# Half-precision pairs for the products with normed activations, their weight scales measured a tile behind, and a piecewise end of the layer outputs

## The chip, the cores and the metric

One core of a Trainium2 chip runs the whole program, four transformer layers in one launch. The metric is the device time of one execution in microseconds. TensorE (PE) does the matrix products, VectorE (DVE) and ScalarE (ACT) the element work, GpSimd (POOL) some of it, SyncE (SP) issues nearly all DMAs.

## What is computed

512 latent tokens of width 1024 pass two layers of a first block and two of a second; in the first layer of the first block 256 context tokens go along, so it works on 768 columns. All in fp32 accuracy. Cut to what the change touches:

```python
# first block, l = 0, 1
u  = modulate(rms_norm(h, g_norm1[l]), ...)            # 1024 wide
pl = u @ w_in[l]                                       # 2720 columns: three kinds of attention
gates = sigmoid(u @ w_gate[l] + b_gate[l])             # 3072 columns
h  = h + mod * (sum(gates * branches) @ w_o[l])
u2 = modulate(rms_norm(h, g_norm2[l]), ...)
h  = h + mod * conv_ffn(u2, w_up[l], ..., w_down[l])   # 5632 up columns, 2816 down rows
# second block, l = 0, 1
proj = rmsnorm(x, attn_norm_w[l]) @ w_in_2[l]          # 2964 columns: state space, short conv, sparse attention
x = x + concat([y_ssd, y_sc, y_nsa]) @ w_out_2[l]
u = causal_dwconv(rmsnorm(x, ffn_norm_w[l]) @ ffn_w_up_2[l], ...)   # 5504 columns
x = x + (silu(gate) * val) @ ffn_w_down_2[l]
```

## The kernel before

Activations lie transposed: 128 rows of d on the partitions (eight tiles for 1024), tokens along the free dimension, in columns 0 to 511 for the latent tokens and 512 to 767 for the context. Below, F0 and F1 are the two layers of the first block (class `First`) and N0 and N1 those of the second (class `Second`).

**Products.** Every dense product is made of three matmuls, since each fp32 operand x is held as a pair of float32r tiles, hi and lo = x - hi: `mm3` (L200) issues wh*xh and wh*xl for all k, then wl*xh. A product of a 128-column weight tile with 1024 rows over 512 tokens is thus 24 matmuls of 512 columns. In the trace a normed activation is `uh`/`ul`, a weight pair `wh`/`wl`, the inner activations of the feed-forward part `hh`/`hl`. The attention weights against values (`pt`, `v`) are fp16 pairs already.

**Weights.** `WS.get` (L660) loads 256 columns (1 MB) into one of two buffers `wr`, and splits 128 columns at a time: ACT copies to `wh`, DVE subtracts to `wl`; there are three buffers of each. In the mixers of the second block (`g.wpool = 1`) POOL does the subtraction.

**Norm.** `Norm.run` (L548) takes a function `tile(k, piece)` that makes output tile k of the preceding product. It does tiles 0 to 6 whole, adding their squares to one sum (`full`); the last tile is done piece by piece of 256 tokens, and after each piece `chain` sums the squares over the partitions on PE, takes the root on POOL, and spreads it over the partitions with PE; `scale` then makes the pairs `uh`/`ul`. `Between` is the norm from F1 to N0 (two norms in one), `Finish` the last one with the output.

**Feed-forward** (`ffn`, L1481). Groups of four 128-row tiles: `up` makes gate and value products (each evacuated by `conv_tile`: one ACT with scale and bias, two DVE taps) and a pair hh/hl; `down` multiplies the group with w_down and adds it to h. Two tiles of the next product are begun piece by piece by `early`. The pair hh/hl lies in ring `K` (14 buffers in the first block, 22 in the second, where h lies in it too).

**Order.** The order of each engine's instructions is that of a scheduler which places them by priority (program order) and a model of times; engines then run in that order, each waiting for what its next instruction needs. Products of mixers are interleaved by `weave` with attention work.

Of the kernel before, what the change touches and what calls it, by code (L numbers as in the profile page):

```python
# [18 lines left out]
P = 128  # L19
# [9 lines left out]
SPLIT = 1  # L29
# [7 lines left out]
SM = 26  # L37
UP, VP = 2.0 ** 14, 2.0 ** 12
LAT = (0, S)
# [26 lines left out]
class Gen:  # L66
    def __init__(self, tc, ins, outs, ctx, dbg=None):
# [4 lines left out]
        self.hold = []  # L72
# [27 lines left out]
    def param(self, shape, dt=F32, name="c"):  # L100
        n = int(np.prod(shape[1:]))
        tag, b = ("K128", 24) if n <= 32 else ("K512", 10)
        assert n <= 128
        return self.cp.tile(shape, dt, name=self.nm(name), tag=tag, bufs=b)
# [23 lines left out]
    def parts(self, n, name):  # L128
# [4 lines left out]
        return out  # L133

# [134 lines left out]

    def stats(self, sq, Dn, ntt, eps=EPS, bank="po", small=False):  # L270
# [187 lines left out]
class Norm:  # L458
    def __init__(self, g, h, n, A, B, parts=THIRDS):
        self.g, self.h, self.n, self.A, self.B = g, h, n, A, B  # L460
        self.u, self.rp, self.acc, self.sq = None, [], {}, {}
        self.tiles = [x for x in parts if x[0] < n]

# [59 lines left out]
    def scale(self, i, ks=range(KD)):  # L523
        g = self.g
        o, w = self.tiles[i]
        if self.u is None:
            self.u = [g.parts(self.n, "u") for _ in self.h]
        rp = self.cols(i)
        for k in ks:
# [5 lines left out]
            if b is None:  # L535
                s = g.act(y, x)
                (g.ptt if k % 3 == 2 else g.tt)(z, x, y.bitcast(F32), OP.subtract)
            else:
                s = g.act(y, x, AF.Identity, bias=b)
                if k % 2 == 1:  # L540
                    g.act(x, x, AF.Identity, bias=b)
                    g.ptt(z, x, y.bitcast(F32), OP.subtract)
                else:
                    g.stt(z, x, b, y.bitcast(F32), OP.add, OP.subtract)
        if i == 0:
            g.hold = [v, s]

    def run(self, tile, segs, split=1):  # L548
# [21 lines left out]
class Between(Norm):  # L570
    def __init__(self, g, h, g1, f):
# [4 lines left out]
        self.A = [gw]  # L576
        self.rs = g.param([P, 4], name="rsk")
# [10 lines left out]

    def chain(self, i, last):
# [3 lines left out]
        qs = [(x, 0, k) for x, k in zip(self.sq.pop(i), last)]  # L593
# [58 lines left out]
class WS:  # L652
# [7 lines left out]
    def get(self, c, M):  # L660
# [30 lines left out]
        out.key = (id(self), c)  # L691
        return out
# [235 lines left out]
class First:  # L928
    def __init__(self, g, l, h, ada_next=None):
# [4 lines left out]
        self.nq = T if self.ctxq else S  # L934

# [71 lines left out]
    def win(self, c0, c1, cc=256):  # L1007
        return self.g.wstream(self.g.I["w_in"][self.l], 0, KD, c0, c1, cc)
# [329 lines left out]
    def gates(self):  # L1338
        g = self.g
        wg = g.wstream(g.I["w_gate"][self.l], 0, KD, 0, 3 * D)  # L1340
        self.th = []

        def one(d):
            th = g.slot("L", "th")
            wt = wg.get(d * P, P)
            for o, wd in self.qsegs:
                ps = yield from g.dense(wt, self.u, (o, wd))
                g.act(th[:, o:o + wd], ps, AF.Tanh, scale=0.5, bias=self.hbg[:, d:d + 1])
# [73 lines left out]
    def project(self, merged, sp):  # L1422
# [9 lines left out]
        h, xs = [], []  # L1432

        def tile(d, sg):
            w, (o, wd) = wo.get(d * P, P), sg
# [6 lines left out]
        return h, Norm(g, h, nq, A, B).run(tile, self.qsegs)  # L1442

    def run(self, ahead, consumer):
# [16 lines left out]
        u = ffn(g, u2, h, self.qsegs, I["w_up"][l], I["w_down"][l], D_FF, self.cw, self.cb, (0, 44 // 2), 1,  # L1461
# [6 lines left out]
def conv_tile(g, ps, seg, out, cw, cb, c, lead, M):  # L1468
    o, w = seg
    nt = len(cw)  # L1470
    g.act(out[:M, o:o + w], ps, AF.Identity, scale=cw[lead][:M, c:c + 1], bias=cb[:M, c:c + 1])
    for j in range(nt):
# [5 lines left out]
        g.stt(x, ps[:, a + d:b + d], cw[j][:M, c:c + 1], x, OP.mult, OP.add)  # L1478


def ffn(g, u, h, segs, w_up, w_down, dff, cw, cb, coff, lead, scale, consumer, ahead):  # L1481
# [3 lines left out]
    wg = g.wstream(w_up, 0, KD, 0, dff)  # L1485
    wv = g.wstream(w_up, 0, KD, dff, 2 * dff)
# [3 lines left out]
    def up(ts):  # L1490
        hs = []
        for p0 in range(0, len(ts), 2):
            pair = ts[p0:p0 + 2]
            gates = []
            for t in pair:
# [3 lines left out]
                for sg in segs:  # L1499
                    conv_tile(g, drain(g.dense(w, u, sg, M)), sg, x, cw, cb, coff[0] + t, lead, M)  # L1500
                g.act(x[:M, :n], x[:M, :n], AF.Silu)
                gates.append(x)
            for t, gt in zip(pair, gates):
# [3 lines left out]
                for sg in segs:  # L1507
                    conv_tile(g, drain(g.dense(w, u, sg, M)), sg, x, cw, cb, coff[1] + t, lead, M)
                g.tt(x[:M, :n], x[:M, :n], gt[:M, :n], OP.mult)
# [6 lines left out]
    def down(ts, hs):  # L1516
        wd = g.wstream(w_down, ts[0] * P, [min(P, dff - t * P) for t in ts], 0, D, 512, 256)

        def tile(d, sg):
            o, wid = sg  # L1520
            ps = drain(g.dense(wd.get(d * P, P), hs, sg))
# [9 lines left out]
    def rest(c, hs):  # L1531
        tile = down(c, hs)
        for d in range(KD):
            for sg in segs:
                tile(d, sg)
# [699 lines left out]
```

## Time and profile before

| | |
|---|---|
| median of 3 runs | 3877.01 us (3876.66 to 3880.73) |
| the profiled execution | 3866.76 us, span 3865.0 us |
| PE, DVE, ACT, POOL busy | 96%, 64%, 46%, 13% of the span |
| mean granted TensorE clock | 0.970 |
| read from HBM, written | 339.32 MB, 38.67 MB |

The profile is read by stage. From the trace's start: F0 mixers to about 866 us, its norm and feed-forward to 1432, F1 mixers 1450 to 2104 and feed-forward 2122 to 2470, N0 mixers 2492 to 2790 and feed-forward 2806 to 3168, N1 mixers 3180 to 3478 and feed-forward 3492 to 3850, then the output. The short stretches between are norms.

### The profile page before, as it was taken

How to read it: one execution, taken by the hardware profiler on the slowest of the kernel's cores; microseconds unless marked ns; L12 is line 12 of the kernel's file. 1: busy time of each engine (PE TensorE's matmuls, PEld its weight loads, DVE VectorE, ACT ScalarE, POOL GpSimd, SP SyncE). 2: the span in 40 equal slices, each digit the busy share in tenths (PEclk: the TensorE clock that was granted, in tenths of full speed). 3: DMA queues.
4: the chain of work that ended last, by engine and by line, in shares of the span. 5: the costliest groups of instructions: out<-in, count | busy, mean ns of one | idle time of the engine just before them, and what ended most of it. 6: DMA issues, size and time to landing. Idle time of an engine off the chain costs nothing. (4 is left out here: it accounts for less than half of the span.)

```text
span 3865.0 us, 54467 instructions
## 1 busy us (share of the span) xinstructions
PE 3704.6 (96%) x20896; PEld 3078.4 (80%) x20896; DVE 2458.5 (64%) x4270; ACT 1794.8 (46%) x3000; POOL 512.0 (13%) x423
## 2 busy tenths in 40 slices
PE   8999999999999999989999999989999998999999
PEld 6888887888888888867767888767788876778886
DVE  5857676656544467668665555678765567876555
ACT  4646666424333236557654333455543335554333
POOL 2101110221000003121112000234100003410000
PEclk9999999999999999999999999989999998999999
DMA  8636898922222225559993322324433322453231
GB/s 246 145 90 153 180 218 226 244 89 79 88 77 87 72 77 131 118 136 216 232 274 126 110 95 93 94 70 104 113 100 98 96 83 67 99 132 98 88 106 60
DMA packets 692255, 483.96 MB, mean 125 GB/s; under 512 B 345790, under 2 KB 620892, under 8 KB 691996
## 3 DMA queue, kind: packets, MB, share of 16 engines
q1 hardware_dynamic: 686172, 468.33, 45.5%
q0 software_dynamic: 5824, 12.15, 1.6%
q8 instruction: 165, 2.70, 0.3%
q14 instruction: 94, 0.77, 0.1%
HBM read 339.32 MB, written 38.67 MB: 98 GB/s over the span
## 5 line engine op out<-in xcount | busy, mean ns | idle before, releaser
L176 ACT ACTIVATE wh<-w 128x1024 fp32r<-128x1024 f32 (+5 forms) x518 | 503.1, 975 | 720.3 <-PE pM L189 232.3
L179 DVE TENSOR_TENSOR wl<-w,wh 128x1024 fp32r<-128x1024 f32 (+3 forms) x464 | 526.0, 1136 | 359.8 <-ACT wh L176 99.7
L189 PE MATMUL pM<-uh,wh 128*128 128x512 f32 (+5 forms) x1832 | 687.2, 381 | 14.6 <-ACT dr L176 9.4
L189 PE MATMUL pM<-ul,wh 128*128 128x512 f32 (+5 forms) x1832 | 662.4, 375 | 0.0
L189 PE MATMUL pM<-uh,wl 128*128 128x512 f32 (+5 forms) x1832 | 450.0, 373 | 0.0
L189 PEld LDWEIGHTS pM<-uh,wh 128*128 128x128 f32 (+3 forms) x1832 | 352.3, 192 | 79.3 <-ACT dr L176 12.7
L189 PEld LDWEIGHTS pM<-ul,wh 128*128 128x128 f32 (+3 forms) x1832 | 343.4, 191 | 56.7
L189 PEld LDWEIGHTS pM<-uh,wl 128*128 128x128 f32 (+3 forms) x1832 | 327.2, 189 | 56.7
L189 PE MATMUL pT<-uh,wh 128*128 128x512 f32 (+3 forms) x912 | 311.1, 353 | 3.0 <-ACT uh L176 2.3
L189 PE MATMUL pT<-ul,wh 128*128 128x512 f32 (+3 forms) x912 | 298.2, 348 | 0.0
L176 ACT ACTIVATE p<-pS,nb 128x768 f32<-128x768 f32 (+7 forms) x304 | 217.6, 716 | 122.4 <-DVE nb L793 116.8
L793 DVE TENSOR_REDUCE nb<-pS 128x1 f32<-128x768 f32 (+7 forms) x304 | 218.0, 725 | 54.6 <-PE pS L189 52.9
L182 DVE SCALAR_TENSOR_TENSOR hl<-p,sm,hl 128x768 f16<-128x768 f32 (+5 forms) x224 | 174.2, 781 | 71.9 <-ACT hl L176 70.4
L176 ACT ACTIVATE hl<-p,sm 128x768 f16<-128x768 f32 (+5 forms) x224 | 159.9, 719 | 108.5 <-DVE sm L1297 26.2
L185 POOL TENSOR_TENSOR rs<-st,half 128x2 f32<-128x2 f32 (+2 forms) x34 | 32.3, 949 | 1327.8 <-DVE st L512 1148.9
L189 PE MATMUL pT<-uh,wl 128*128 128x512 f32 (+3 forms) x912 | 205.3, 351 | 0.0
L185 POOL TENSOR_TENSOR wl<-w,wh 128x1024 fp32r<-128x1024 f32 (+1 forms) x54 | 129.6, 2404 | 537.6 <-ACT wh L176 421.6
L189 PEld LDWEIGHTS pT<-uh,wh 128*128 128x128 f32 (+2 forms) x912 | 171.4, 188 | 28.8 <-ACT uh L176 4.3
L189 PE MATMUL po<-pt,v 128*128 128x128 f16 (+1 forms) x1656 | 174.8, 250 | 16.6 <-DMA pt<-hl 13.0
L189 PEld LDWEIGHTS pT<-ul,wh 128*128 128x128 f32 (+2 forms) x912 | 166.7, 186 | 22.5
L189 PEld LDWEIGHTS <-v 128*128 128x128 f16 x1656 | 123.3, 101 | 60.9 <-issue 43.8
L189 PEld LDWEIGHTS pT<-uh,wl 128*128 128x128 f32 (+2 forms) x912 | 153.8, 188 | 21.9 <-issue 0.4
(581 smaller groups left out, 7763.0 us busy)
## 6 DMA issues: line engine op xcount, KB each, us to landing
w<-w_up SPq DMA_DIRECT2D x44, 1024.0 KB
aw<-w_ada SPq DMA_DIRECT2D x40, 1024.0 KB
w<-ffn_w_up SPq DMA_DIRECT2D x40, 1024.0 KB
w<-w_in SPq DMA_DIRECT2D x70, 512.0 KB
w<-w_gate SPq DMA_DIRECT2D x24, 1024.0 KB
w<-w_down SPq DMA_DIRECT2D x20, 1024.0 KB
ld<-spill SPq DMA_DIRECT2D x51, 384.0 KB
w<-ffn_w_down SPq DMA_DIRECT2D x16, 1024.0 KB
```

The costliest lines, as they stand in the source:

```text
L176: return self.nc.scalar.activation(out, in_, func, **kw)
L179: return self.nc.vector.tensor_tensor(out, a, b, op=op)
L182: return self.nc.vector.scalar_tensor_tensor(out, a, s, b, op0=op0, op1=op1)
L185: return self.nc.gpsimd.tensor_tensor(out, a, b, op=op)
L189: return self.nc.tensor.matmul(out, l, r, start=start, stop=stop)
L793: nc.vector.tensor_reduce(nb, ps, axis=AX.X, op=OP.max, negate=True)
```

## The change

Four things. (1) In F1, N0 and N1 the norms write their pairs in fp16, scaled so that their bound fits (`Norm.fit`, factor `inv`), and w_in, w_gate, w_up are split into fp16 pairs scaled by a constant over the root of a bound on the matrix's sum of squares (`WS16`); the scale is undone where a product is evacuated (`dense_raw`, `conv_tile` through scaled taps, `hf`). F0, w_o, w_down, w_branch, w_out and the head products stay float32r pairs. hi and lo of a weight tile lie in one buffer, so the six buffers hold six weight tiles. (2) The scale needs the sum of squares of each weight matrix, so it is read once more ahead of its use: `Measure.steps` loads pieces of 128 rows by up to 768 columns into ring `K`, two after each tile of a feed-forward part (`next(g.slow)`), and squares or takes the maximum of each one step later, two of three on ACT, one on DVE, placed behind the last evacuation (`behind`). F1's matrices (46.8 MB) are measured in F0's feed-forward part, N0's (34.7 MB) in F1's, N1's (34.7 MB) in N0's. (3) Ahead of the four norms that follow a feed-forward part, four output tiles instead of one are done piece by piece (`SPLIT = 4`), in the second block's middle norms two instead of one. (4) In the mixers of the second block the weight subtraction goes from POOL to DVE, products rotate over pM, pT, pM (four banks) instead of pM (two), and `conv_silu` evacuates by `conv_tile` straight from PSUM instead of from a copy.

```diff
-SPLIT = 1
+SPLIT = 4
@@ Gen
+    def parts16(self, n, name):
+        lat = self.t("U", [P, S], F32, name).bitcast(F16)
+        if n == S:
+            return [lat[:, :S], lat[:, S:]]
...
     def dense_raw(self, wp, x, segs, M=P, r0=0, tag="R"):
+        f = getattr(wp, "f", None)
...
-            self.act(out[r0:r0 + M, sg[0]:sg[0] + sg[1]], ps)
+            self.tail[0] = self.act(o, ps) if f is None else self.act(o, ps, AF.Copy, scale=f[:M])
@@ Norm
+    def fit(self, gain):
...
+        for v in range(n):
+            nc.vector.tensor_reduce(m[:, v:v + 1], gain[v], axis=AX.X, op=OP.max, apply_absolute_value=True)
...
+        ps = g.bank("po")
+        for v in range(n):
+            g.mm(ps[:, :1], mb[:, v:v + 1].to_broadcast([P, P]), g.onesb[:, :1], v == 0, v == n - 1)
...
+    def part(self, k, i, key=0, scale=None):
+        g = self.g
+        o, w = self.tiles[i]
+        a = self.acc[key][:, o:o + w]
+        (g.ptt if key else g.tt)(a, a, self.square(k, o, w, scale), OP.add)
     def run(self, tile, segs, split=1):
...
                 for k in last:
                     tile(k, self.tiles[i])
-                self.sq[i] = [self.square(k, *self.tiles[i]) for k in last]
+                    if k < KD - 1:
+                        self.part(k, i)
+                self.sq[i] = [self.square(KD - 1, *self.tiles[i])]
+class Measure:
...
+    def behind(self, e, f):
+        g = self.g
+        with ExitStack() as st:
+            if g.tail[e] is not None:
+                st.enter_context(g.tc.issue_after(g.tail[e].ins))
+            f()
+    def steps(self):
...
+        def square(i, x):
+            g.act(x, x, AF.Square, accum_out=acc[:, i:i + 1])
+        def largest(i, x):
+            a = acc[:, i:i + 1]
+            nc.vector.tensor_reduce(a, x, axis=AX.X, op=OP.max, apply_absolute_value=True)
+            g.tt(a, a, a, OP.mult)
+        for i, (k, a, b) in enumerate(cuts):
+            x = g.slot("K", "wm")[:, :b - a]
+            nc.sync.dma_start(x, self.w[k * P:(k + 1) * P, a:b])
+            todo.append((i, x))
+            if len(todo) == 2 or i == n - 1:
+                yield
+                for j, y in todo:
+                    e = int(j % 3 == 2)
+                    self.behind(e, lambda: (square, largest)[e](j, y))
+                todo = []
...
+class WS16:
...
+    def split(self, raw, n):
+        g = self.g
+        g.ws += 1
+        pr = g.t("wh" if g.ws % 2 else "wl", [P, 2, KD, n], F16, "w2")
...
+            g.act(pr[:, 0], raw, AF.Copy, scale=self.m.s)
+            g.stt(pr[:, 1], raw, self.m.s, pr[:, 0], OP.mult, OP.subtract)
@@ ffn, after each tile of up and each d of a group's down
+                next(g.slow, None)
...
+    drain(g.slow)
     out = consumer(h).run(down(cs[-1], b), segs, SPLIT)
@@ Second
     def conv_silu(self, c, j, tag):
-        ps = yield from g.dense_raw(self.win(c, c + P).get(c, P), self.u, [LAT])
+        ps = yield from g.dense(self.win(c, c + P).get(c, P), self.u, LAT)
...
-        g.wpool = 1
+        g.wpool, g.banks = 1, MB
...
-        u2 = Norm(g, h, S, [self.gf], None).run(tile, [LAT])
+        nm = Norm(g, h, S, [self.gf], None, half=True)
+        u2 = nm.run(tile, [LAT], 2)
```

## Rows read from the trace of the kernel before

**Rows 1.** The page, busy time of each engine (share of the span, instructions).
```profile
PE 3704.6 (96%) x20896; PEld 3078.4 (80%) x20896; DVE 2458.5 (64%) x4270; ACT 1794.8 (46%) x3000; POOL 512.0 (13%) x423
```

**Rows 2.** Windows: length, busy time of each engine, clock, DMA share, GB/s.
```profile
core 0: us, PE busy (x) PEld busy (x) DVE busy (x) ACT busy (x) POOL busy (x), PEclk, DMA share, GB/s
881.00:1432.00 551.00, 551.00 (x3274) 483.36 (x3273) 294.47 (x435) 178.39 (x230) 4.60 (x5) 1.00 0.25 81
1432.00:1450.00 18.00, 15.84 (x105) 14.91 (x104) 11.73 (x35) 8.37 (x17) 4.32 (x6) 0.72 0.28 85
1450.00:2104.00 654.00, 611.94 (x3671) 498.40 (x3671) 443.59 (x798) 362.47 (x614) 123.98 (x113) 0.97 0.74 180
2122.00:2470.00 348.00, 347.00 (x1536) 287.39 (x1537) 205.05 (x263) 135.30 (x168) 6.67 (x5) 1.00 0.31 99
2470.00:2492.00 22.00, 15.12 (x90) 11.16 (x89) 14.85 (x48) 8.65 (x19) 9.09 (x11) 0.69 0.23 70
2492.00:2790.00 298.00, 269.86 (x1567) 218.88 (x1565) 222.07 (x425) 153.45 (x313) 92.25 (x53) 0.93 0.41 99
2790.00:2806.00 16.00, 13.49 (x95) 12.30 (x95) 13.61 (x35) 8.51 (x18) 5.13 (x6) 0.89 0.02 2
2806.00:3168.00 362.00, 359.47 (x1569) 288.10 (x1568) 205.27 (x270) 133.67 (x170) 0.00 (x0) 1.00 0.32 98
3168.00:3180.00 12.00, 9.64 (x57) 7.87 (x56) 7.59 (x25) 4.87 (x11) 5.18 (x5) 0.72 0.23 66
3850.00:3865.00 15.00, 7.31 (x53) 6.56 (x52) 3.56 (x7) 3.58 (x7) 1.40 (x2) 0.69 0.38 140
```

**Rows 3.** Timeline of PE: start us, us, operation, count of equal neighbours merged.
```profile
2496.62 1.12 PE L189 MATMUL pT<-ul,wh 128*128 128x256 f32 x8
2909.87 1.98 PE L189 MATMUL pT<-uh,wl 128*128 128x512 f32 x8
...
1515.60 2.14 PE L189 MATMUL po<-pt,v 128*128 128x256 f16 x18
1886.13 1.18 PE L189 MATMUL po<-pt,v 128*128 128x128 f16 x18
```

**Rows 4.** Windows again, of the instructions on tile uh alone, from F1 on.
```profile
1440.00:3865.00 2425.00, 1192.39 (x4016) 729.18 (x4016) 35.77 (x68) 43.81 (x104) 30.38 (x36) 0.96 0.44 117
2122.00:2470.00 348.00, 207.87 (x672) 126.17 (x672) 0.00 (x0) 0.00 (x0) 0.00 (x0) 1.00 0.31 99
2806.00:3168.00 362.00, 209.03 (x680) 125.35 (x679) 1.29 (x4) 0.81 (x2) 0.00 (x0) 1.00 0.32 98
```

**Rows 5.** Timeline of PE about the norm from N0 to N1, idle time before in brackets.
```profile
3169.47 1.05 PE L189 MATMUL po<-ones,sq 128*128 128x1 f32 x8
...
3175.49 0.44 PE L189 MATMUL pT<-uh,wh 128*44 128x256 f32 x1 [0.53 <-ACT uh L176]
```

**Rows 6.** Mixers of N0: a wait of PE, and timelines of POOL and DVE.
```profile
PE pM L189 <- ACT dr L176: 5.4, 3, 4.9
...
2502.53 5.20 POOL L185 TENSOR_TENSOR wl<-w,wh 128x1024 fp32r<-128x1024 f32 x2 [9.92 <-ACT wh L176]
...
2505.39 2.38 DVE L1618 TENSOR_SCALAR gates<-gates 128x48 f32<-128x48 f32 x1
2508.45 0.17 DVE L1623 TENSOR_SCALAR dz<-dx 128x32 f32<-128x32 f32 x1
```

**Rows 7.** Groups by shape over the whole trace: busy us, mean ns | idle before.
```profile
L176 ACT ACTIVATION_READ_ACCUMULATOR p<-pS,nb 128x1 f32 x304 | 58.7, 193 | 0.0
L176 ACT ACTIVATE sq<-h 128x768 f32<-128x768 f32 x22 | 18.6, 844 | 16.9 <-DVE h L182 16.7
L176 ACT ACT_TABLE_LOAD x10 | 12.8, 1283 | 2.5 <-DVE gt L182 1.6 <-PEq L2225 0.7
L179 DVE TENSOR_TENSOR wl<-w,wh 128x1024 fp32r<-128x1024 f32 x394 | 488.2, 1240 | 312.4 <-ACT wh L176 95.0 <-PE pM L189 78.4 <-PE pT L189 65.8
L793 DVE TENSOR_REDUCE nb<-pS 128x1 f32<-128x768 f32 x128 | 120.5, 950 | 22.9 <-PE pS L189 22.2
```

**Rows 8.** Waits of SP's queue in N0's feed-forward part: us in total, times, longest.
```profile
SPq L669 <- DVE wl L179: 307.2, 33, 20.1
```

More of the change, by code (lines that the diff above doesn't have):

```diff
@@ L592, in chain @@
         o, w = self.tiles[i]
-        qs = [(x, 0, k) for x, k in zip(self.sq.pop(i), last)]
+        qs = [(x, 0, KD - 1) for x in self.sq.pop(i)]
         for tt in range(2):
@@ new lines, with __init__, load, get @@
+class WS16:
+    def __init__(self, g, w, m, c0, c1, cc):
+        self.g, self.w, self.m, self.c1, self.cc = g, w, m, c1, cc
+        self.rawr = self.curr = (0, 0)
+    def load(self, c):
+        g = self.g
+        e = min(c + self.cc, self.c1)
+        self.raw = g.t("wr", [P, KD, e - c], F32, "w")
+        g.last = g.nc.sync.dma_start(self.raw, self.w[:, c:e].rearrange("(k p) n -> p k n", p=P))
+        self.rawr = (c, e)
+    def split(self, raw, n):
+        g = self.g
+        g.ws += 1
+        pr = g.t("wh" if g.ws % 2 else "wl", [P, 2, KD, n], F16, "w2")
+        with ExitStack() as after:
+            g.soft -= 1
+            for x in g.hold if g.soft >= 0 else ():
+                after.enter_context(g.tc.issue_after(x.ins))
+            g.act(pr[:, 0], raw, AF.Copy, scale=self.m.s)
+            g.stt(pr[:, 1], raw, self.m.s, pr[:, 0], OP.mult, OP.subtract)
+        return pr
+    def get(self, c, M):
+        if not (self.curr[0] <= c and c + M <= self.curr[1]):
+            if not (self.rawr[0] <= c < self.rawr[1]):
+                self.load(c)
+            e = min(c + P, self.rawr[1])
+            o = c - self.rawr[0]
+            self.cur, self.curr = self.split(self.raw[:, :, o:o + e - c], e - c), (c, e)
+        return self.pack(self.cur, c - self.curr[0], M, (id(self), c))
+    def pack(self, pr, o, M, key):
+        out = Wt((pr[:, 0, k, o:o + M], pr[:, 1, k, o:o + M]) for k in range(KD))
+        out.key, out.f = key, self.m.f
@@ L1007, in win, with measures, ready @@
     def win(self, c0, c1, cc=256):
-        return self.g.wstream(self.g.I["w_in"][self.l], 0, KD, c0, c1, cc)
+        g, w = self.g, self.g.I["w_in"][self.l]
+        return g.wstream16(w, self.ms["in"], c0, c1, cc) if "in" in self.ms else g.wstream(w, 0, KD, c0, c1, cc)
+    def measures(self, names):
+        g, l, I = self.g, self.l, self.g.I
+        ws = {"in": (I["w_in"], 2720), "gate": (I["w_gate"], 3 * D), "up": (I["w_up"], 2 * D_FF)}
+        for n in names:
+            self.ms[n] = Measure(g, ws[n][0][l], ws[n][1])
+            yield from self.ms[n].steps()
+    def ready(self, inv):
+        g = self.g
+        for n in ("in", "gate"):
+            self.ms[n].factor(inv)
+        f = self.ms["gate"].t[:, 5:6]
+        g.nc.vector.tensor_scalar(f, self.ms["gate"].f, 0.5, None, op0=OP.mult)
+        self.hf = f
     def groups(self, lat):
@@ L1441, in project @@
         A, B = self.mods(2)
-        return h, Norm(g, h, nq, A, B).run(tile, self.qsegs)
+        m = self.ms.get("up")
+        nm = Norm(g, h, nq, A, B, half=bool(m))
+        u = nm.run(tile, self.qsegs)
+        if m:
+            m.factor(nm.inv)
+        return h, u
     def run(self, ahead, consumer):
@@ L1535, in rest @@
                 tile(d, sg)
+            next(g.slow, None)
     for c in cs[:-2]:
@@ L1548, in __init__, with measures, ready @@
         self.g, self.l, self.h = g, l, h
-        self.ws = {}
+        self.ws, self.ms = {}, {}
+    def measures(self):
+        g, l, I = self.g, self.l, self.g.I
+        for n, w, c in (("in", I["w_in_2"], 2964), ("up", I["ffn_w_up_2"], 2 * D_FF_2)):
+            self.ms[n] = Measure(g, w[l], c)
+            yield from self.ms[n].steps()
+    def ready(self, inv):
+        g = self.g
+        self.f = f = self.ms["in"].factor(inv)
+        self.hf = self.ms["in"].t[:, 5:6]
+        g.nc.vector.tensor_scalar(self.hf, f, 0.5, None, op0=OP.mult)
+        for x in self.hcw:
+            g.nc.vector.tensor_scalar(x, x, f, None, op0=OP.mult)
     def params(self):
```

154 lines of the change are left out of this document (114 added, 40 removed).

## The prediction

> **What bounds the kernel now.** I read the page first: PE is busy for 96% of the span, the next engine, DVE, for 64% [rows 1]. Such a share is an average, so the windows by stage come next [rows 2]. In the feed-forward parts PE is busy without a gap at a granted clock of 1.00 (551.0 of 551 us in F0, 347.0 of 348 in F1, 359.5 of 362 in N0; N1 is like N0): these stages last as long as their matmuls take, and ACT and DVE wait there. In the mixers PE is busy for 94% (F1) and 91% (N0, and N1 the same), the rest being chains through ACT, DVE and POOL. In the norms between stages PE idles, and the clock then falls to its lower level, 1.2 instead of 2.4 GHz: a clock of 0.72 over 18 us means that 0.28 of the stretch was lost twice over, 5 us of work. So three things can gain: fewer ns per matmul, in full only in the feed-forward parts; less idle time at the norms; a looser chain in the mixers.
>
> **Part 1, the type of the products.** No matmul is added or removed; only the step from one to the next can change. In a merged row the step is (row's length - length of one) / (count - 1), with 0.39, 0.28 and 0.23 us for one of 512, 256 and 128 columns. Float32r: (1.98 - 0.39) / 7 = 227 ns at 512 columns, (1.12 - 0.28) / 7 = 120 at 256 [rows 3]. Fp16: (2.14 - 0.28) / 17 = 109.4 at 256, (1.18 - 0.23) / 17 = 55.9 at 128 [rows 3]. No fp16 matmul of 512 columns is in the trace. Its two ends: 512 columns at 2.4 GHz, 213 ns, and twice the 256-column step, 219. I take the line through the two fp16 rows, 109.4 + 2 x 53.5 = 216.4, so each product saves 10.6 ns (8 to 14); at 256 columns the rows give the same, 120 - 109.4 = 10.6.
>
> The Trainium skill, "TensorE: Matmul & The Clock Gate", section "Back-to-back issue gap", gives N / 2.4 + 2.5 ns per matmul at the higher clock and names no type; that is 216 ns at 512 columns for either, and by it alone the new type would save nothing. The trace agrees for fp16 and differs for float32r, whose rows read 227; the rows decide.
>
> How many: `uh` stands in 4016 matmuls from F1 on [rows 4], `ul` in half as many (two hi products for each lo one), 6024 in all. F1's up has 672 x 1.5 = 1008, N0's and N1's 680 x 1.5 = 1020 each, together 3048: x 10.6 ns = 32 us, all of it on the path, as PE is the bound there. The other 2976, in mixers and norms, give at most 31.5 us. Part of that turns into waits for the attention chains, so I take three quarters, 24 (bounds 0 and 31.5).
>
> **Part 2, the end of the layer outputs.** A piece of the last output tile of a feed-forward part covers 12 matmuls, 1.4 us; four tiles cover 48 x 0.120 = 5.8 us. The chain behind a piece is 3169.47 to 3175.49, 6.0 us from the sums to the first product with the new activation [rows 5]. So the chain of all pieces but the last comes to lie beneath products, and PE has the first pieces' products to do while the last one's chain runs. What is there to win is idle time plus clock [rows 2]: F0 to F1 2.2 + 5.0; F1 to N0 6.9 + 6.8; N0 to N1 2.4 + 3.4; middle norm of N0 2.5 + 1.8, N1 counted the same. Together 35 us. The 4.4 us of added cover takes most of it where the chain is one, half where it is two norms long (F1 to N0): 5 + 7 + 4.5 + 2.5 + 2.5. At the end, 3850 to 3865, the first piece's output work moves beneath products: 2 us of 15. Sum 24 (bounds 12 and 35).
>
> Its price: a 512-column product becomes two of 256, 2 x 120 - 227 = 13 ns more, for 4 x 36 + 2 x 24 = 192 products: 2.5 us.
>
> **Part 3, the mixers of N0 and N1.** Four banks instead of two, and no copy ahead of the convolution, remove the wait of PE for that copy: 5.4 us in N0, 4.9 of it once [rows 6]. But the bank is now freed by the third DVE tap and not by ACT. I take half, 2.5 us a layer, 5 in all (bounds 0 and 15 for both, the rest of the chain loosening with it).
>
> The 21 subtractions of N0 that POOL did in 2.5 us each go to DVE at 1.24 [rows 7]: 26 us more on an engine busy for 222 of 298 [rows 2]. What it gets back: while POOL runs two of them from 2502.53 to 2507.73, a DVE operation on 48 elements begun at 2505.39 takes 2.38 us, to 2507.77; its like, a little later, takes 0.17 [rows 6]. I take the two as equal, cost nil; bounds -8 and +13 us a layer.
>
> The Trainium skill, "SBUF — State Buffer", section "Who interferes with whom", calls what the two share an exclusive port pair: whichever of a GpSimd read and a DVE operation with two SBUF inputs comes first blocks the other for its whole length. The row above ends with POOL's, as the rule has it. Against the change the rule says that POOL's remaining work (rotary products) now waits behind DVE's longer subtractions.
>
> **Part 4, the measuring.** Each weight matrix is read once more: pieces of 1/8 of its rows, 128 (64 steps) in F0's feed-forward part, 96 (48) in F1's, 136 (68) in N0's. A piece on ACT costs 0.844 + 0.193 us for the sum's read, on DVE 0.950 [rows 7]. F0: 85 x 1.04 = 88 us of ACT, 43 x 0.95 = 41 of DVE; their idle time there is 373 and 257 [rows 2]. F1: 66 and 30 against 213 and 143. N0, narrower pieces: at most 94 and 44 against 228 and 157. ACT's table is loaded 10 times in the whole run, though squares and Silu alternate between stages [rows 7], so Square needs no load of its own. All this hides beneath PE; were it not hidden, it would be some 360 us.
>
> The transfers: F1's part takes 34.7 MB in about 52 of 80 steps, 226 us: 153 GB/s beside the 99 of now. That row has a DMA share of 0.31 at 99 [rows 2], so 252 is about 0.79: near full, not over. F0 comes to 178 GB/s, N0 to 204. Weights come early enough now, since SP waits not for landings but for a free weight buffer, 307 us in N0's part [rows 8].
>
> What is added are waits: ACT's and DVE's next evacuation is queued behind a measuring operation whose piece may not have landed; PE waits for the evacuation once its five or six banks are full. SP holds weight loads behind a piece that waits for a buffer of ring K. No row shows such a wait. Below it is bounded by 0, above by the rival below; I take 10 us, mainly for F1's part.
>
> Small work: seven measures and five fits each put one tiny product on PE behind a short DVE chain, at most one idle of the kind in [rows 5], 0.53 us: 6 us at most, 2.5 taken. The scale as an operand on ACT and DVE lies in their idle time.
>
> **The sum.** 32 + 24 + 24 + 5 - 10 - 2.5 - 2.5 = 70 us. The profiled execution, 3866.8 us (span 3865.0), becomes 3796.8. The median is 10.2 us above it, with the same work; off the median it is 3877 - 70 = 3807.
>
> **The rivals.**
> - The mixers give nothing back, since their chains set the pace, and the norms half: 32 + 12 - 10 - 5 = 29, 3848 us (3830 to 3866). For it: PE idles 9% in N0's mixers while DVE is at 75%. Against: F1's mixers, with over half of these products, are at 94% PE.
> - More comes: mixers in full, all the idle time and clock of the norms, the looser chain 15, no measuring wait: 32 + 31.5 + 35 + 15 - 5 = 108, 3769 us (3745 to 3785). For it: every clock loss in [rows 2] follows a short idle.
> - Slower: measuring operations at the head of ACT's and DVE's queues wait for pieces still in flight. It decides from a mean loss for PE of 0.44 us a step on (80 us over 180 steps). At 0.6 us it is 108 in place of 10: 3877 - 80 + 108 = 3905 us. For it: in a down step of F1's part, 12 x 0.227 = 2.7 us, two pieces (0.73 MB) and weights (0.26 MB) ask for 364 GB/s, above the 319 to which that row's share extends. Against: outside the down steps the demand is below it, and the banks hold four tiles.
> - The change of type doesn't do what it says, 512-column fp16 stepping like float32r: 3807 + 56 = 3863 us. For it: no fp16 matmul of 512 columns stands in the trace, so the 216 is a line drawn on; against it: 256 columns in [rows 3]. (The formula of the Trainium skill cited in part 1 also gives this.)
>
> **How the numbers follow.** The forecast, 3785 to 3830, has 0.57; gives nothing back 0.18; more 0.10; slower 0.11; no gain of type 0.04. A measurement of this kernel can tell about 0.2%, 8 us, from no change. Below 3869 lie all of the first and third, nearly all of the second and most of the fourth: faster 0.87; slower 0.10; the strip between takes 0.03. The range 3762 to 3866 leaves out the slower case, and edges of two others, about 0.16.
>
> **What would show it.** Right: merged rows of 512-column products on `u` step by 216 ns; the feed-forward parts of F1, N0, N1 are each 10 to 11 us shorter, F0's the same; norms show a clock above 0.85 and under 2 us idle; ACT and DVE show squares of `wm` in three feed-forward parts with PE still at 99%. Wrong: PE idle there ended by ACT or DVE operations that themselves waited for a `wm` transfer, or by weight loads that landed late; DVE over 90% busy in the mixers of N0 with PE idle more than the 28 us of now; steps of 227 ns with fp16.

## The result and the profile after

The change takes 3826.28 us (median of 4 runs, 3821.61 to 3833.07) where the kernel before takes 3876.84 (3869.80 to 3880.73): a ratio of 0.9873, 95% interval 0.9852 to 0.9894, or 50.6 us less. On a second chip it was 3822.69 against 3866.23, a ratio of 0.9885 (0.9870 to 0.9901). The forecast was 3807, 70 us less, in a range of 3762 to 3866. So the direction and the range held, and 19 to 26 us of the gain are missing. The profiled execution has a span of 3824.2 us, 40.8 less than that of before.

The page's busy times after, which answer to [rows 1]: PE has 68 us less to do, DVE 108 and ACT 180 more.

```profile
PE 3637.0 (95%) x21103; PEld 2603.6 (68%) x21103; DVE 2566.9 (67%) x4682; ACT 1974.5 (52%) x3490; POOL 405.0 (11%) x389
```

To see where the 40.8 us lie I cut both traces at the same events: a stage ends with the last product on `sq` (the sums of squares) of a norm. So the rows are, in order: F0's feed-forward part, F1's mixers, F1's feed-forward part with most of the norm to N0, N0's mixers, its feed-forward part, N1's mixers, its feed-forward part. First before, then after; columns as in [rows 2].

```profile
core 0: us, PE busy (x) PEld busy (x) DVE busy (x) ACT busy (x) POOL busy (x), PEclk, DMA share, GB/s
865.14:1442.76 577.62, 574.39 (x3430) 505.35 (x3431) 314.16 (x484) 194.41 (x261) 12.76 (x15) 0.99 0.25 80
1442.76:2102.13 659.37, 617.13 (x3701) 503.56 (x3698) 449.04 (x811) 367.73 (x625) 126.21 (x116) 0.96 0.74 179
2102.13:2476.09 373.96, 368.12 (x1683) 307.07 (x1683) 222.60 (x305) 152.35 (x200) 18.89 (x17) 0.99 0.31 98
2476.09:2791.49 315.40, 281.28 (x1623) 226.47 (x1622) 235.39 (x468) 159.48 (x327) 97.43 (x60) 0.91 0.40 95
2791.49:3171.82 380.33, 375.29 (x1675) 302.13 (x1675) 219.42 (x304) 143.63 (x189) 6.35 (x6) 0.99 0.31 94
3171.82:3478.37 306.55, 278.66 (x1611) 226.37 (x1610) 230.36 (x445) 158.81 (x325) 97.92 (x60) 0.92 0.39 96
3478.37:3854.84 376.47, 374.62 (x1693) 302.87 (x1692) 218.05 (x297) 149.75 (x203) 4.91 (x6) 1.00 0.27 85
```

```profile
870.14:1447.02 576.88, 573.58 (x3476) 505.79 (x3476) 354.25 (x604) 266.59 (x443) 14.47 (x18) 1.00 0.47 162
1447.02:2104.22 657.20, 606.08 (x3697) 407.76 (x3695) 455.54 (x826) 372.90 (x624) 127.35 (x116) 0.95 0.73 179
2104.22:2485.27 381.05, 363.64 (x1724) 217.51 (x1725) 265.06 (x402) 207.19 (x339) 20.12 (x22) 0.97 0.57 193
2485.27:2782.57 297.30, 267.34 (x1647) 173.83 (x1645) 226.43 (x492) 154.03 (x317) 40.35 (x38) 0.93 0.38 95
2782.57:3152.91 370.34, 364.91 (x1717) 214.99 (x1716) 256.74 (x425) 200.90 (x376) 6.57 (x8) 0.99 0.60 193
3152.91:3444.44 291.53, 265.76 (x1635) 167.44 (x1633) 218.71 (x474) 154.55 (x316) 42.02 (x37) 0.95 0.39 98
3444.44:3814.89 370.45, 366.30 (x1736) 216.47 (x1736) 222.25 (x304) 151.12 (x207) 5.73 (x6) 1.00 0.28 88
```

Length less PE's busy time is PE's idle time in a stage. Three things stand out. F1's mixers lose 2 us of length although PE has 11 us less to do: idle time grows from 42 to 51. F1's feed-forward stage grows by 7 us, with idle time from 6 to 17. And N0's and N1's mixers lose 18 and 15, more than the type can give them. F0's mixers, with the same instructions on PE, POOL and SP in the same order in both kernels, took 865.1 and 870.1 us: so without this stage the two executions differ by 46 us and not by 40.8.

The type itself did what it should. A merged row of 24 products on `u` with 512 columns, from F1's feed-forward part (start, length, operation, count): (5.34 - 0.38) / 23 = 215.7 ns, where [rows 3] gave 227 for float32r.

```profile
2265.55 5.34 PE L197 MATMUL po<-u,w 128*128 128x512 f16 x24
```

What goes wrong is seen best at the norm from F1 to N0. First PE's longest waits there, before and after (us in total, times, longest), then the timeline of ACT and DVE after:

```profile
PE pS L189 <- DVE st L600: 1.6, 1, 1.6
PE po L197 <- DVE st L659: 6.0, 1, 6.0
```

```profile
2477.06 1.15 ACT L184 ACTIVATE w<-w,wsc 128x1024 f16<-128x1024 f32 x1 [1.59 <-DMA w<-w_in]
...
2476.85 0.16 DVE L187 TENSOR_TENSOR st<-rsk 128x2 f32<-128x2 f32 x1 [0.60 <-POOL rsk L193]
2478.24 1.28 DVE L190 SCALAR_TENSOR_TENSOR w<-w,wsc,w 128x1024 f16<-128x1024 f32 x1 [1.23 <-ACT w L184]
2479.45 0.68 DVE L187 TENSOR_TENSOR st<-st 128x2 f32<-128x2 f32 x1
...
2480.39 0.15 DVE L659 TENSOR_SCALAR st<-st 128x2 f32<-128x2 f32 x1
```

DVE is in the middle of the norm's chain (`st`, on 2 elements) when its next instruction is half of a weight split, whose other half stands on ACT, which waits for a transfer of N0's weights. The chain goes on at 2479.45, 2.4 us later; that is the split's part of PE's 6.0 us, and the rest is the chain itself and the additions of squares between its steps. That split is the fourth of its stream, and the first products on `u` don't use it. Before, three pairs of weight buffers held the weights, and by then only two splits of this size had been made; with hi and lo in one buffer there are six. The same in N0's middle norm, where nothing is in flight: ACT's and DVE's rows, then what PE waited.

```profile
2789.13 4.25 ACT L184 ACTIVATE w<-w,wsc 128x1024 f16<-128x1024 f32 x4
2792.10 5.70 DVE L190 SCALAR_TENSOR_TENSOR w<-w,wsc,w 128x1024 f16<-128x1024 f32 x4
2793.74 0.38 PE L197 MATMUL pM<-u,w 128*128 128x256 f16 x2 [1.92 <-ACT u L184]
2798.19 0.59 PE L197 MATMUL pM<-u,w 128*128 128x512 f16 x2 [1.24 <-DVE u L187]
```

Four splits in a row hold ACT for 4.25 us and DVE for 5.70, and the norm's second piece of `u` waits behind them. Before, single splits stood there, and the two waits were 0.52 and 0.47 us.

### The profile page after: what moved, and what is told of

It is laid out like the page before. It is cut to its first block, busy times and chain, and to the rows that moved or that the text cites. A ratio compares the mean times of both kernels' runs of the same rounds, so it can differ in the third digit from the quotient of the medians.

```text
span 3824.2 us, 56251 instructions
## 1 busy us (share of the span) xinstructions
PE 3637.0 (95%) x21103; PEld 2603.6 (68%) x21103; DVE 2566.9 (67%) x4682; ACT 1974.5 (52%) x3490; POOL 405.0 (11%) x389
## 5 line engine op out<-in xcount | busy, mean ns | idle before, releaser
L197 PEld LDWEIGHTS <-w 128*128 128x128 f16 (+3 forms) x6024 | 589.0, 100 | 651.7 <-issue 73.8
L197 PE MATMUL pM<-u,w 128*128 128x512 f16 (+3 forms) x3096 | 690.7, 373 | 23.3 <-ACT u L184 12.5
L197 PE MATMUL pT<-u,w 128*128 128x512 f16 (+3 forms) x1920 | 415.6, 364 | 7.6 <-DVE xd L187 3.6
L184 ACT ACTIVATE wh<-w 128x1024 fp32r<-128x1024 f32 (+5 forms) x288 | 262.7, 917 | 292.6 <-PE pM L197 79.3
L187 DVE TENSOR_TENSOR wl<-w,wh 128x1024 fp32r<-128x1024 f32 (+5 forms) x278 | 301.3, 1087 | 152.3 <-ACT wh L184 67.1
L190 DVE SCALAR_TENSOR_TENSOR w<-w,wsc,w 128x1024 f16<-128x1024 f32 (+1 forms) x230 | 293.2, 1290 | 100.5 <-ACT w L184 100.1
L184 ACT ACTIVATE w<-w,wsc 128x1024 f16<-128x1024 f32 (+1 forms) x230 | 254.9, 1132 | 170.0 <-DMA w<-ffn_w_up 67.3
L197 PE MATMUL pM<-uh,wh 128*128 128x512 f32 (+2 forms) x720 | 248.1, 357 | 1.7 <-ACT uh L184 0.9
L197 PE MATMUL pM<-ul,wh 128*128 128x512 f32 (+2 forms) x720 | 241.0, 352 | 0.4 <-POOL ul L193 0.4
L184 ACT ACTIVATE wm<-wm 128x501 f32<-128x501 f32 (+6 forms) x243 | 174.6, 721 | 30.4 <-DMA wm<-w_up 10.2
```

The lines of the kernel that those rows point to most:

```text
L184: return self.nc.scalar.activation(out, in_, func, **kw)
L187: return self.nc.vector.tensor_tensor(out, a, b, op=op)
L190: return self.nc.vector.scalar_tensor_tensor(out, a, s, b, op0=op0, op1=op1)
L197: return self.nc.tensor.matmul(out, l, r, start=start, stop=stop)
```

## The experiments

All stage lengths below are cut as above. Ratios are to the kernel before, measured beside each.

**The change without its pieces.** Part 2 undone.

```diff
-SPLIT = 4
+SPLIT = 1
...
-        u2 = nm.run(tile, [LAT], 2)
+        u2 = nm.run(tile, [LAT])
```

> The changed kernel with part 2 undone: SPLIT is 1 again, and the middle norms of N0 and N1 do one tile in pieces. Stages are counted from the last sum-of-squares product of one norm to that of the next. The cover theory, that of the prediction: four tiles in pieces hide the chains, so without them about 24 us come back, 3826 to 3850 us. The chain theory, read from the trace after: at F1 to N0 the pieces make the chain longer (PE idle 12.3 of 26 us there, against 6.9 of 22 before), and elsewhere they bring nothing, so F1's feed-forward stage falls from 381 to about 372 us, the other norms stay within 2 us each, and the whole is 3814 to 3820 us.

Ratio 0.9893 (0.9880 to 0.9907), 3827.98 us: neither the 24 us of the cover nor a gain. F1's feed-forward stage came to 370.2 us, as the chain theory had it, but N0's feed-forward stage came to 379.2 in place of 370.3, and N1's mixers took 306.6 in place of 291.5. And PE's longest wait from F1 to N0 was still 5.6 us, so the pieces aren't its cause.

**One norm in one piece.** Only the norm from F1 to N0 goes back to one tile in pieces.

```diff
     def run(self, *a):
-        super().run(*a)
+        super().run(*a[:2])
```

> The changed kernel with one thing undone: at the norm from F1 to N0 one tile is done in pieces, and not four. The cover theory (the prediction gave this norm 7 us): F1's feed-forward stage grows from 381 to about 388 us, the whole to 3833. The chain theory: the stage falls to about 372, the whole to about 3817; this one norm is then all of what undoing the pieces everywhere brings.

Ratio 0.9900 (0.9887 to 0.9914), 3830.91 us; F1's feed-forward stage 377.1, between the two theories, and the longest wait there 6.4 us. Both theories fail: with pieces or without, this wait stays. Something that all kernels with fp16 weights share must make it.

**The change without the measuring.** `Measure.steps` sets a constant scale.

```diff
-        for i, (k, a, b) in enumerate(cuts):
...
+        nc = self.g.nc
+        nc.vector.memset(self.s, 2.0 ** 9)
+        nc.vector.memset(self.r, 2.0 ** -9)
         yield
...
```

> The changed kernel without the measuring: the second reading of the weights, their squares and maxima are left out, and the scale is a constant, 512. If the measuring costs what the prediction put down for it (10 us, mainly in F1), F1's feed-forward stage falls from 381 to about 373 us (PE waits about 5 us from 2158 to 2166 us, and its clock is low for 6.8 us behind that), N0's stays at 370, and the whole is 3814 to 3818. If the waits in F1's part come from the order of the evacuations alone, nothing changes: 3826 within 5. If pieces in flight held back more than the trace shows, F0's part (577 us) and N0's fall too, by 3 us or more each.

Ratio 0.9871 (0.9858 to 0.9885), 3818.84 us. F1's feed-forward stage 376.4 (381.1 and 380.1 in two executions of the change), F0's 576.2 (576.9, 576.5), N0's 369.9 (370.3, 370.5): some 5 us by stage, which is too little to be seen in the ratio. The wait from F1 to N0 stays, 5.9 us. So does the first down product's wait at the start of F1's part, which I had put down to the measuring. PE's row there in the change, and here:

```profile
2161.53 0.47 PE L197 MATMUL po<-hh,wh 128*128 128x512 f32 x1 [2.91 <-DVE gt L190]
```

```profile
2159.08 0.76 PE L197 MATMUL po<-hh,wh 128*128 128x512 f32 x1 [3.44 <-DVE gt L190]
```

**Part 3 alone**, on the kernel before.

```diff
-        ps = yield from g.dense_raw(self.win(c, c + P).get(c, P), self.u, [LAT])
+        ps = yield from g.dense(self.win(c, c + P).get(c, P), self.u, LAT)
...
-        g.wpool = 1
+        g.banks = MB
         weave(g, [first, s0, s1] + hs)
-        g.wpool = 0
```

> The kernel before with part 3 alone: in the mixers of N0 and N1 the weight subtraction goes to DVE, products rotate over four banks, and the convolution evacuates from PSUM. The prediction: 2.5 us a layer, 3877 to 3872, and N0's mixers 315 to 313 us, N1's 307 to 304. The theory from the two traces: the change of type can give these stages only 624 products x 10.6 ns = 6.6 us each, of 18 and 15 that they lost, so part 3 gives 8 to 11 a layer: 3877 to about 3857, N0's mixers about 305, N1's about 298. If the gain there belongs to the type (shorter products that loosen the chain), the two stages stay within 2 us of 315 and 307.

Ratio 0.9965 (0.9952 to 0.9978), 13.0 us: between the 5 of the prediction and the 20 of the theory from the two traces. The windows of N0's and N1's mixers:

```profile
2477.16:2785.21 308.05, 278.29 (x1623) 224.43 (x1622) 226.55 (x492) 155.00 (x319) 33.28 (x34) 0.91 0.39 97
3163.60:3464.17 300.57, 274.06 (x1610) 224.76 (x1609) 219.34 (x469) 155.29 (x317) 32.31 (x32) 0.92 0.39 97
```

They lose 7.3 and 6.0 us. PE's wait of 5.4 us in N0 for the copy `dr` [rows 6] is gone, and in its place is one for the third tap of the convolution:

```profile
PE pM L189 <- DVE xc L182: 2.8, 1, 2.8
```

And DVE, which took 21 subtractions of 128 x 1024 (1.25 us each) and 5 of 128 x 768 (0.95) from POOL in N0, 31 us, is busy for 226.6 us and not 235.4. One operation of it in N0's mixers, with the same operands in both kernels, shows why: its group before and then here (count, busy us, mean ns).

```profile
L182 DVE SCALAR_TENSOR_TENSOR xc<-xt,xc 128x512 f32<-128x512 f32 x8 | 7.3, 919 | 2.7 <-ACT xt L176 2.7
```

```profile
L182 DVE SCALAR_TENSOR_TENSOR xc<-xt,xc 128x512 f32<-128x512 f32 x8 | 5.5, 688 | 1.5 <-ACT xt L176 1.5
```

The mean of 919 ns hides two kinds. Seven of the eight took 680 to 695 ns, as all eight do here; one took 2.51 us: it began while POOL was in a subtraction, which lasted to 2548.00, and ended 0.56 us behind that. An undisturbed one, that one, and POOL's row, from the trace of before:

```profile
2527.48 0.69 DVE L182 SCALAR_TENSOR_TENSOR xc<-xt,xc 128x512 f32<-128x512 f32 x1
2546.05 2.51 DVE L182 SCALAR_TENSOR_TENSOR xc<-xt,xc 128x512 f32<-128x512 f32 x1
2545.46 2.54 POOL L185 TENSOR_TENSOR wl<-w,wh 128x1024 fp32r<-128x1024 f32 x1
```

In N0's mixers before, 31 operations of DVE that overlapped POOL's work took 38.7 us longer in sum than the shortest of their kind; with part 3 alone 14 did, by 9.8 us.

**The change once more.** The same kernel, for what a stage differs by on its own.

> The changed kernel as it is, once more, beside the next ones, for what a stage differs by from one execution to the next with the same order of instructions. The mixers of F0, the same instructions in the same order in both kernels, took 865.1 and 870.1 us, so I expect up to 5 us there, 1 us in the feed-forward stages, and 3 us in F1's mixers (657 us); the ratio to before again 0.987.

Ratio 0.9885 (0.9870 to 0.9901), 3822.69 us. All 21103 matmuls come in the same order as in the first trace, and each stage but F0's mixers (868.3 against 870.1) is within 1.5 us of the first. So I take a difference of 3 us in a stage to mean something, and one of 3 us in the whole not to; two executions are few for such a bound.

**Three buffers.** fp16 weight tiles take one of the two buffer names in place of both by turns.

```diff
-        pr = g.t("wh" if g.ws % 2 else "wl", [P, 2, KD, n], F16, "w2")
+        pr = g.t("wh", [P, 2, KD, n], F16, "w2")
```

> The changed kernel with three buffers for fp16 weight tiles in place of six. Theory of the buffers: with hi and lo in one buffer the planner splits up to six weight tiles ahead, and the splits behind the third stand in ACT's and DVE's queues in front of a norm's own operations (four in a row, 4.3 us of ACT and 5.3 of DVE, in the middle norms; ACT waiting for a transfer of w_in ahead of the last squares from F1 to N0, where PE idles 6.1 us in a piece in every kernel with fp16 pairs, with pieces or without). With three buffers that idle falls from 6.1 to under 2 us, F1's feed-forward stage from 381 to 370 to 374, the middle norms lose 1 to 2 us each, and the whole is about 3812. Theory that the idle comes from the measuring or from the type: no change of these (3826 within 5). Rival: the shallower stock costs more in the mixers than it gives at the norms, 3830 or above, with PE idle in N0's mixers above 33 us.

Ratio 0.9846 (0.9829 to 0.9862), 3803.48 us, 19 us less than the change beside it: faster than both kernels. From F1 on, stage by stage:

```profile
1443.49:2089.57 646.08, 603.58 (x3698) 404.29 (x3695) 456.29 (x826) 374.60 (x625) 126.90 (x116) 0.96 0.76 183
2089.57:2464.48 374.91, 361.48 (x1725) 217.19 (x1726) 260.79 (x399) 204.31 (x336) 20.51 (x22) 0.97 0.56 192
2464.48:2764.58 300.10, 269.73 (x1646) 175.10 (x1644) 226.60 (x495) 156.43 (x320) 42.52 (x38) 0.91 0.39 99
2764.58:3135.51 370.93, 366.25 (x1716) 215.55 (x1717) 255.69 (x424) 199.58 (x374) 7.29 (x8) 0.99 0.58 192
3135.51:3423.81 288.30, 266.69 (x1635) 169.57 (x1633) 218.06 (x474) 155.88 (x318) 43.82 (x37) 0.94 0.40 100
```

F1's feed-forward stage is at 374.9, just above the range expected, and the longest wait from F1 to N0 only fell to 3.7 us and not under 2. The middle norm of N0 has single splits again (ACT's rows), and PE's wait in it is 0.77 us:

```profile
2771.12 1.14 ACT L184 ACTIVATE w<-w,wsc 128x1024 f16<-128x1024 f32 x1
2772.36 2.37 ACT L184 ACTIVATE u<-ut 128x256 f16<-128x256 f32 x6
2775.52 1.15 ACT L184 ACTIVATE w<-w,wsc 128x1024 f16<-128x1024 f32 x1 [0.78 <-DVE w L190]
2777.38 0.38 PE L197 MATMUL pM<-u,w 128*128 128x256 f16 x2 [0.77 <-ACT u L184]
```

What I hadn't put into the numbers is the largest part: F1's mixers lose 11 to 13 us, to 646. There a score bank `pS` is free when ACT has done its exponentials `p`. PE's waits for that in F1's mixers, in the order before, the change, four buffers (below), three:

```profile
PE pS L189 <- ACT p L176: 7.5, 4, 5.7
```

```profile
PE pS L197 <- ACT p L184: 16.8, 10, 3.9
```

```profile
PE pS L197 <- ACT p L184: 8.8, 10, 1.4
```

```profile
PE pS L197 <- ACT p L184: 1.0, 2, 0.8
```

In the change's timeline of ACT one such place reads:

```profile
1914.85 2.19 ACT L184 ACTIVATE w<-w,wsc 128x1024 f16<-128x1024 f32 x2 [5.34 <-DMA w<-w_gate]
1916.95 1.26 ACT L184 ACTIVATE qs<-ld 64x512 fp32r<-64x512 f32 x2
1918.24 0.80 ACT L184 ACTIVATE p<-pS,nb 128x641 f32<-128x641 f32 x1
```

ACT waits 5.34 us for a transfer of gate weights, splits two tiles of them, and the exponentials come after that.

**Six buffers, splits held back.** The first split after the first two tiles of a stage stands behind the norm's first piece, the next three behind its last.

```diff
-SPLIT = 4
+SPLIT, HB = 4, 4
...
+        g.hold2 = [v, s]
...
-            for x in g.hold if g.soft >= 0 else ():
+            g.behind2 -= 1
+            for x in () if g.behind2 < 0 else g.hold if g.behind2 == HB - 1 else g.hold2:
                 after.enter_context(g.tc.issue_after(x.ins))
```

> The changed kernel, six buffers, but of the weight splits that follow the first two tiles of a stage the first is placed behind the norm's first piece, the next three behind its last piece. Theory of the buffers: the splits leave the norm's way, PE's idle of 6.1 us from F1 to N0 falls below 2 us, F1's feed-forward stage to 370 to 374, the middle norms lose 1 to 2 us each, 3810 to 3815. Theory that depth is needed at the start of a stage: PE waits for the third and fourth weight tile behind each norm instead, and the whole stays at 3826 within 5.

Ratio 0.9901 (0.9885 to 0.9917), 3829.70 us. At five of the six norms it did what it should: no wait of 6 us is left, F1's feed-forward stage takes 371.7 us and N0's 366.6, 9 and 4 less. From F0 to F1 PE idles longer, 7.4 us in place of 3.9, and 2.6 of these it waits for a split of weights (ACT `w`), as the second theory had it. And F1's mixers, which begin there, take 668.4, 10 to 11 more, with PE idle for 62 us: what was won at the norms went there. The order of the rest of the stage was changed by it too, so beyond that wait this run doesn't say by what.

**Fewer gate products.** The third part of each gate product of F1's mixers (low part of the weight times `u`) is left out.

```diff
+            wt.two = half
...
-            self.mm(ps, wh, xl, False, False)
+            self.mm(ps, wh, xl, False, two and i == n - 1)
             yield
+        if two:
+            return
```

> The changed kernel with the third part of each gate product of F1's mixers (low part of the weight times u) left out: 192 matmuls of 512 columns, 192 x 216 ns = 41.5 us of PE. If PE sets the pace of that stage, it falls from 657 to about 616 us. If chains of the attention set it, as the type's 15.5 us that only gave 2 there would say, it falls by less than a quarter of that, to 647 or more, and PE idles some 35 us longer. In between, at 630, both.

Ratio 0.9839 (0.9816 to 0.9861), 3803.61 us of two runs. The stage took 636.0 us, 21 to 23 less than the change's 657.2 and 658.6, of 41.5 us of PE work taken away; PE idles 68 us in place of 51. Half of this saving on PE comes out of the stage, half turns into waiting. The matmuls that are left come in another order, though (2210 of 3504 stand as in the change), so this isn't the chains' part alone.

```profile
1443.10:2079.10 636.00, 568.08 (x3505) 389.40 (x3504) 459.17 (x826) 372.81 (x624) 127.17 (x116) 0.95 0.76 185
```

**Three buffers, one norm in one piece** (the two diffs above together).

> Three buffers for fp16 weight tiles, and the norm from F1 to N0 in one piecewise tile (the other norms as in the change). With three buffers and four tiles in pieces PE still idles 9.2 us from the sums there to the first product on u, since 8 additions of POOL (0.7 us each) and as many of DVE stand between the steps of its chain. If these additions are what is left, the idle of that norm comes down to the 6.9 us of before, F1's feed-forward stage from 375 to 371 or less, and the ratio to before from 0.985 to 0.983. If the cover of the pieces is worth more than they cost, the stage grows by 3 us or more.

Ratio 0.9866 (0.9849 to 0.9883), 3815.22 us. The norm did as expected: F1's feed-forward stage 371.0, the longest single wait there 1.4 us. But N0's mixers took 305.1 (300.1) and N1's 297.1 (288.3). In N1's only 1437 of 1633 matmuls stand in the same order as with three buffers alone, while F1's mixers, where all 3695 do, differ by 1.3 us. An edit at one norm had the planner order the later stages anew, and that cost more than the edit gave.

**Three buffers, no pieces.**

> Three buffers, and one tile in pieces everywhere (part 2 undone, free of the effect of the six buffers). The prediction's cover, 24 us: ratio to before 0.991, the norm from N0 to N1 and the middle norms longer by 3 to 5 us each. What the stages showed so far: from F1 to N0 3 us shorter, from N0 to N1 5 to 9 us longer, the middle norms 1 us, so a sum of about 5 to 8 us, ratio 0.986 to 0.987. Pieces worth nothing: 0.985.

Ratio 0.9849 (0.9832 to 0.9866), 3811.69 us: no difference from three buffers with pieces (0.9846) that could be told. N1's feed-forward stage, the cleanest for the type, took 364.9 us, against 367.8 with pieces:

```profile
3436.70:3801.60 364.90, 362.84 (x1692) 211.84 (x1692) 218.17 (x297) 150.86 (x203) 5.96 (x6) 1.00 0.27 88
```

**Four buffers.**

```diff
-        pr = g.t("wh" if g.ws % 2 else "wl", [P, 2, KD, n], F16, "w2")
+        pr = g.t("wh" if g.ws % 4 else "wl", [P, 2, KD, n], F16, "w2")
```

> Four weight tiles instead of three or six. If every further tile that the planner splits ahead costs alike at the norms and in F1's mixers, this lies a third of the way from three (ratio 0.985) to six (0.989): 0.986, F1's mixers 650 us, PE's longest idle from F1 to N0 4.5 us. If a fourth tile is a gain (a stock against late transfers) and only the bunching of four splits in a row costs, it is as fast as three or faster, 0.984 or less. If any stock over three lets the planner put splits ahead of the norm, 0.988.

Ratio 0.9864 (0.9841 to 0.9887), 3817.09 us. F1's mixers 656.4 us and the wait from F1 to N0 6.3 us are those of six; the middle norm of N0 is mended (idle 1.1 us). So in those two places it isn't a cost per tile: four buffers are as slow as six there. The ratio lies between those of three and six, and its interval takes in both.

**Three buffers, no measuring.**

> Three buffers and no measuring: the second reading of the weights, their squares and maxima are left out, and the scale is a constant, 512. With six buffers the constant scale took 4.6 us off F1's feed-forward stage, and 0.7 and 0.5 us off F0's and N0's. If that is what the measuring costs, the same comes off here: F1's stage from 375 to about 370, ratio to before from 0.985 to 0.983. If the waits there came from the order that the six buffers gave, nothing changes with three: the stage within 1.5 us of 375, ratio 0.985. If the measuring costs the 10 us of the prediction, 0.982.

Ratio 0.9814 (0.9798 to 0.9831), 3795.40 us. The stages with measuring in them lose 0.9 (F0), 5.5 (F1, to 369.4) and 3.5 us (N0, to 367.5), 9.9 together; the ratio's difference, 0.0032, is 12 us. The rest of the whole moved as well (N0's mixers 4.8 less, N1's 3.7 more), so the 9.9 too hold what a new order gives or takes.

PE's idle time at the six norms (not the one in F0), from 4 us ahead of the products on `sq` (in the middle norms, of the last of them) to 17 us behind the last, summed from PE's timeline (with no pieces, 1.6 us of the wait from F1 to N0 lie ahead of that):

| us | F0 to F1 | F1 | F1 to N0 | N0 | N0 to N1 | N1 | sum |
|---|---|---|---|---|---|---|---|
| before | 2.2 | 3.2 | 6.9 | 2.5 | 2.4 | 2.1 | 19.3 |
| the change | 3.9 | 4.0 | 12.2 | 4.2 | 4.0 | 4.4 | 32.6 |
| no pieces | 3.2 | 4.4 | 8.5 | 4.4 | 5.4 | 4.4 | 30.2 |
| splits held back | 7.4 | 3.1 | 8.1 | 2.2 | 1.3 | 2.3 | 24.4 |
| four buffers | 4.4 | 3.3 | 11.0 | 1.1 | 2.9 | 2.0 | 24.6 |
| three buffers | 3.0 | 3.1 | 9.5 | 2.0 | 3.7 | 2.3 | 23.6 |
| three, no pieces | 2.1 | 4.7 | 7.0 | 2.3 | 4.2 | 2.3 | 22.6 |

## Why the prediction was right, and where it was wrong

**The type in the feed-forward parts (32 us): right.** The step is 215.7 ns, where 216.4 was forecast. N0's and N1's stages lose 10.0 and 6.0 us in the change; in the cleanest case, N1's with three buffers and no pieces, 376.5 to 364.9, it is 11.6 us, and 1104 products (early ones among them) x 10.6 ns are 11.7. F1's stage kept nothing of it: what it gave went into the norm behind it and into waits inside the stage, 5.1 us where there were 1.7. So of the prediction's signs, 10 to 11 us less in each of the three stages, one came in the change itself. With that step the rival of no gain from the type is gone.

**The mixers (24 of 31.5 us): about right in sum, by two errors.** F1's mixers, which the prediction held for the safest since PE is busy there for 94%, gave 2.2 us in the change (0.8 in its second execution) of 15.5 (1464 products x 10.6 ns). With three buffers they gave 13.3. N0's and N1's gave 10.7 and 9.0 on top of part 3 alone, above the 6.6 each that the products make; the clock in them rose (0.91 to 0.93, 0.92 to 0.95, though only to 0.93 in N1's second execution, which was as short), and the rest may be the planner's order, which no run here tells apart. What the rival "the mixers give nothing back, and the norms half" says of the mixers thus held for F1's in the change. But it isn't the attention chains alone that set the pace there, as that rival has it: with three buffers, and the same chains, most of the gain came out.

**The norms (24 us): wrong, the step that failed.** Idle time there didn't go, it grew from 19.3 to 32.6 us. The signs it named, under 2 us idle at a norm and a clock above 0.85, fail too: the shortest idle time in the change is 3.9 us, and the clock between 2467 and 2493 us is 0.69. The prediction reckoned how much matmul work the pieces put above the chain of [rows 5], and took that chain to be as long as before. It was not: the change gives the weights six buffers, which the section on the change says and the prediction puts at no cost, and the planner fills them by splits that stand in ACT's and DVE's queues ahead of the norm's squares and products, some waiting for a transfer. Two edits show it: with six buffers and the splits held back the sum is 24.4, and with three buffers 23.6, where F1's mixers get their gain back too and the whole is 19 us less. Both stay above the 19.3 of before. For F1's mixers the order of the matmuls differs as well (2547 of 3695 in the same order), so whether it is the waits at the queue's head or the new order in which they stand is not separated; that six, four and three buffers give 657, 656 and 646 us speaks for the buffers, and 652.8 with three and no pieces is a case between.

And the pieces themselves bring nothing that could be told: with three buffers 23.6 us of idle with them and 22.6 without. From F1 to N0, where the squares of two norms are added on POOL and DVE piece by piece, undoing them there takes 3 us off the norm. So the 24 us were too much even without the buffers; their price, 2.5 us for narrower products, is seen in N1's feed-forward stage alone as 2.9, of which 0.9 come back at the output, where 2 were forecast.

**Part 3 (5 us): right in sign, too small.** 13 us alone. The prediction took half of one wait's removal, and that came so: 5.4 us went, 2.8 came for the third tap. It put DVE's side at nil, bounds -8 and +13 us a layer; the blocked time fell by 29 us in N0 (38.7 to 9.8) for 31 of subtractions taken over, and DVE's busy time fell by 8.8. So N0's stage lost some 5 us more than the one wait explains. Which of the three edits of part 3 gave them, no run separates.

**The measuring (10 us of waiting): about half of it in the change.** It costs some 5 us by stage there, with six buffers, and 9.9 with three. In the change PE isn't idle for it in the inner part of N0's stage (the row below), and in F1's it waits for 5.1 us, of which 2.9 stand without any measuring too. The rival "slower" needs 80 us of such loss, and is far off.

```profile
2798.20:3149.00 350.80, 350.80 (x1614) 203.74 (x1613) 238.40 (x378) 190.07 (x356) 1.10 (x2) 1.00 0.61 198
```

**What this makes of the sum.** Of 70 us forecast the norms' 24 are gone, and 13 us of added idle time there and 8 of clock come on top (61 us at the lower level in those stretches against 44, half of the difference lost). F1's mixers gave 9 us less than their share of the mixers' 24, N0's and N1's 10 more; part 3 gave 8 more, and the measuring took 5 less. That is 70 - 24 - 13 - 8 - 9 + 10 + 8 + 5 = 39 us, beside 46 between the two profiled executions without F0's mixers. The sum is rough, as the norms' cuts overlap the stages', and 7 us stay open. The direction rested on terms that held: the type in stages bound by PE, and measuring in idle time.

## What to carry to other kernels

When a change frees memory and a pool of buffers grows by it, price the growth as an edit of its own: on engines that run in order, work done ahead for later stands in front of what is needed now, and waits there for its transfer. After any edit in a kernel with a planned order compare stages, and within them the order of instructions: an edit at the norm from F1 to N0 moved N1's mixers by 9 us here, as much as the effects that were sought. Of work saved on the bounding engine count all in stages without idle time. Where 6 to 9% of a stage is idle, what comes out depends on the order as much as on the chains: of 15.5 us saved in F1's mixers 2 came out with six buffers and 13 with three, of 41.5 us half. And look at the single rows behind a mean: 919 ns was seven operations of 0.69 us and one of 2.5.

## What was not expected of the hardware

POOL's subtractions of 128 x 1024 elements in N0's mixers held up operations of DVE that met them, until the subtraction ended (2.51 us in place of 0.69), and left the others as they were; so 31 us of added work left DVE busy for 9 us less. The Trainium skill, "SBUF — State Buffer", section "Who interferes with whom", has the two block each other; the runs agree. This operation has two SBUF inputs (`xt`, `xc`), as the rule is put in the prediction; the row on `gates` that stands beside it there has only one. F0's mixers, where matmuls and POOL's operations come in the same order in every kernel, took 864.5 to 870.1 us over all kernels, more than any other stage differed by between two executions of one instruction order (1.5 us); they are part of why the whole scatters by some 10 us.
